# A 32-byte filler tile behind the small constants of a fused two-layer decoder trunk

## The chip, the cores and the metric

The kernel runs on one core of one Trainium2 chip. The metric is the device time of one execution in microseconds (us); a lower number is better. Times are medians of several executions. The profile is of one execution, recorded by the hardware profiler.

## The reference

The program computes two decoder layers over 1,024 tokens of width 1,024, all in float32. The first layer mixes tokens with a gated linear recurrence (HGRN2), the second with sliding-window attention of 16 query heads on 4 key/value heads; each is followed by a gated feed-forward network with a causal convolution of width 3, and every sub-layer ends in a residual sum and a layer norm:

```
for layer in range(DEPTH):                       # DEPTH = 2
    if layer < N_A_LAYERS:
        mix = hgrn2_mixer(h, hgrn_w_in[layer], lower_bounds[layer], hgrn_gnorm_w[layer], hgrn_w_out[layer])
    else:
        mix = swa_sink_mixer(h, k_shared, v_shared, swa_w_q[j], swa_sinks[j], bias, mask, swa_w_out[j])
    h = layer_norm(ALPHA * h + mix, ln_mix_g[layer], ln_mix_b[layer])
    ff = conv_ffn(h, ffn_w_in[layer], ffn_conv_w[layer], ffn_conv_b[layer], ffn_w_out[layer])
    h = layer_norm(ALPHA * h + ff, ln_ffn_g[layer], ln_ffn_b[layer])
    if layer == N_A_LAYERS - 1:
        k_flat, v_flat = jnp.split(h @ shared_w_kv, 2, axis=-1)

def conv_ffn(h, w_in, conv_w, conv_b, w_out):    # w_in (1024, 5632), w_out (2816, 1024)
    u = causal_depthwise_conv3(h @ w_in, conv_w) + conv_b
    a, b = jnp.split(u, 2, axis=-1)
    return (jax.nn.silu(a) * b) @ w_out
```

## The kernel before, in words

**Matmuls.** A float32 product is made of three fast ones. Each operand is kept as a high and a low part (the high part is a rounded copy that ScalarE, ACT in the profile, makes in `split`, L218, or `split_into`, L173; the low part is the difference that VectorE, DVE, makes in `low_part`, L166). `mm3` (L190 to L193) then issues high times high (L191), high times low (L192) and low times high (L193) into one accumulator in PSUM. So nearly all work of TensorE (PE) stands on these three lines. Each matmul first loads 128 stationary columns ("PEld" in the profile) and then streams a moving operand of 512 columns (256 in the projection of values and gates) past them. The loads of the next matmul run while the current one streams.

**Tiles.** [...] The first pool, `cp`, holds what lives for the whole program. The built program has these start addresses (bytes in the partition):

| tile | start | start modulo 64 | holds |
|---|---|---|---|
| `T` | 1,152 | 0 | the activations turned, high and low parts, 64 KB |
| `Y` | 66,688 | 0 | the activations by token, and scratch, 32 KB |
| `HL` | 99,456 | 0 | weights, high and low parts, twelve rows of 4 KB |
| `ident`, `nhalf`, `par`, `cwt`, `lbt`, `msk` | from 148,608 | 0, and 32 for `par` | identity, small constants, masks |
| tiles of `sm` | from 151,072 | 0 or 32 | small statistics of layer norm and softmax |
| all later tiles | from 152,032 | 32 | see below |

The later tiles are declared stage by stage and reuse the same space. The recurrence has `raw0` to `raw2` (landing places of weights), `V`, `G`, `A`, `Ab`, `kp`, `qp`, `kd`, `St` and others; attention has `Kh`, `Kl`, `Vt`, `X`, `q`, `W0`; the feed-forward network has `HT` (three more rows of weights, 12 KB, used like `HL`), `rx0` to `rx2` (landing places of weights), `TX` (48 KB of combined activations, three slots of high and low parts) and, in its second half, `R` and `rd`. Each of them that is 4 KB or larger starts at 32 modulo 64, and every slice of them that a matmul takes is a multiple of 512 bytes further on. The slices of `T`, `Y` and `HL` start at 0 modulo 64 in the same way.

**Order of work.** TensorE's order is written out by hand. `out_proj` (L299) multiplies the mixer's output with its output weights in two halves of 512 columns: in the first, `T` is stationary and `HL` moving, and in the second `T` is stationary and `TX` moving (the weights of `out_late` are laid into `TX` first). Then class `Up` makes the up-projection with seven block products where plain block multiplication needs eight. It loops over 22 columns of blocks `fc`. In each, `weights(fc)` loads blocks of weights into `rx` or `Y`, makes sums of them on DVE (L422 to L425) and splits them into rows of `HL` and `HT`; then seven products of twelve matmuls run in the order 1, 2, 6, 7, 4, 5, 3, each with weights stationary and activations moving. Products 1, 2, 4 and 5 stream `T`, and products 6, 7 and 3 stream `TX`. The stationary operand of 1, 2, 4 and 5 is always in `HL`; that of 6 and 7 is in `HT` when `fc` is even and in `HL` when it is odd, and that of 3 is in `HT` for every third `fc`:

```
for p in (1, 2, 6, 7, 4, 5, 3):
    self.collect(p, fc, self.product(p, fc, banks[n % 8]))
...
ws = [whole((0 if fc % 2 else 8) + i) for i in range(6)] + [whole((14, 6, 7)[fc % 3])]
```

In the last line rows up to 11 are in `HL`, and 12, 13 and 14 are in `HT`. `collect` (L444 to L476) adds the products up in `Y` on DVE and applies the convolution (L468 on ACT, L470 on DVE), the gate and the store.

Class `Down` makes the down-projection with the same seven-product scheme. There one slot of 8 KB holds both operands of a step, so that the stationary and the moving operand always come from the same tile: one of six slots of `HL`, one of `HT`, or eight of `T`, used in turn.

**Engines around it.** DVE, ACT and POOL take their instructions in the order that a scheduler or the code sets; the SP queue issues nearly all DMAs. None of this looks at an address.

Of the kernel before, what the change touches and what calls it, by code (L numbers as in the profile page):

```python
# [10 lines left out]
F32 = mybir.dt.float32  # L11
# [5 lines left out]
P = 128  # L17
# [90 lines left out]
def trunk(ctx: ExitStack, tc: tile.TileContext, a: dict, out: bass.AP):  # L108
# [5 lines left out]
    cp = ctx.enter_context(tc.tile_pool(name="cp", bufs=1))  # L114
# [11 lines left out]
    cwt = cp.tile([P, 2, 4, 2 * NF], F32, name="cwt")  # L126
    lbt = cp.tile([P, 2, NH], F32, name="lbt")
    msk = cp.tile([P, 7 * BL + P], U8, name="msk")
    h2d = drp.tile([P, 8, D], F32, name="h2d")
    ynd = drp.tile([P, 8, D], F32, name="ynd")  # L130
    gd = drp.tile([P, NF, S], F32, name="gd")
# [1347 lines left out]
def build(arrays):  # L1479
    import concourse.bacc as bacc  # L1480

    nc = bacc.Bacc("TRN2", target_bir_lowering=False, num_devices=1, dynamic_dma_scratch_size=1024)
    aps = {n: nc.dram_tensor(f"in_{n}_dram", v.shape, mybir.dt.from_np(v.dtype), kind="ExternalInput").ap()
           for n, v in arrays.items()}
    out = nc.dram_tensor("out_0_dram", (1, S, D), F32, kind="ExternalOutput").ap()
    with tile.TileContext(nc) as tc, tc.manual_schedule(engines={mybir.EngineType.PE}):
        trunk(tc, aps, out)
    return nc
# [10 lines left out]
```

## Time and profile before

| | |
|---|---|
| median of 3 runs | 2186.32 us (2185.72 to 2187.77) |
| span of the profiled execution | 2184.9 us, from its first to its last instruction |
| PE busy | 2164.9 us, 99% of the span, 13,188 matmuls |
| DVE, ACT, POOL busy | 1762.3 us (81%), 893.8 us (41%), 120.3 us (6%) |
| mean granted TensorE clock | 0.998 |
| DMA | 279.05 MB, mean 128 GB/s |

Of the profiled execution the record gives the span and no device time of its own; the median of the runs is 1.4 us above the span.

The program runs through the recurrence (0 to about 500 us of the span), its output projection (to about 577), the first up-projection (to about 1,000) and down-projection (to about 1,180), keys, values and attention (to about 1,455), and then the second output projection, up-projection (to about 1,960) and down-projection.

How to read the rows: a group of matmuls is named `line PE MATMUL out<-in`, with the two SBUF tiles that it reads, the moving one first (`TX,HL` streams `TX` past columns of `HL`; one name alone means that both are slices of that tile); the accumulator is `psmm` or `psax`. Its columns are the count, the busy time in us and the mean duration of one in ns. Matmuls are pipelined, so a duration (some 390 ns) is longer than the distance from one start to the next (some 227 ns); the distance is what adds up to the span. In a timeline the columns are start and duration in us. In rows of waits the columns are total us, times and the longest.

### The profile page before, as it was taken

Reading aid. Unit: us, or ns where it says so; the run is one execution under the profiler, and the core shown is the slowest. Engines: PE = TensorE matmul, PEld = TensorE weight load, DVE = VectorE, ACT = ScalarE, POOL = GpSimd, SP = SyncE. Lnnn points to the kernel's source line nnn. Section 1 sums busy time; section 2 is a strip of 40 time slices with the busy share of each in tenths; the row PEclk is TensorE's granted clock in tenths of the full one; section 3 lists DMA queues with packets and bytes.
Section 4 is the critical chain, followed back from the end, with each engine's and each line's share of the span. In section 5 each row is a group of like instructions: output and inputs, shape, how many; then the busy total and the mean of one; then the engine's idle time right before and its main releaser. Section 6 shows DMA issues by size and latency. Waiting matters only on the chain.

```text
span 2184.9 us, 33220 instructions
## 1 busy us (share of the span) xinstructions
PE 2164.9 (99%) x13188; PEld 1811.8 (83%) x13188; DVE 1762.3 (81%) x2388; ACT 893.8 (41%) x1457; POOL 120.3 (6%) x135
## 2 busy tenths in 40 slices
PE   9999999999999999999999999999999999999998
PEld 8888888898878888888888888878888888888887
DVE  3776665667999988888978568969999988878986
ACT  3233333342444444344433256743544444444430
POOL 1000000000100000000001123211000000000001
PEclk9999999999999999999999999999999999999999
DMA  5654533305223222228854411133223222249762
GB/s 197 232 169 161 183 136 101 99 21 175 98 75 106 87 78 81 83 97 263 290 183 155 126 32 28 32 108 115 87 96 96 79 87 77 78 139 325 235 204 94
DMA packets 229844, 279.05 MB, mean 128 GB/s; under 512 B 29960, under 2 KB 158648, under 8 KB 226872
## 3 DMA queue, kind: packets, MB, share of 16 engines
q1 hardware_dynamic: 228736, 276.53, 38.8%
q8 instruction: 104, 1.70, 0.3%
q10 hardware_dynamic: 856, 0.37, 0.1%
q14 instruction: 52, 0.43, 0.1%
q0 software_dynamic: 96, 0.02, 0.0%
HBM read 213.94 MB, written 62.94 MB: 127 GB/s over the span
## 4 chain that ended last, share of the span: by engine, by line
PE 95%; DVE 4%; ACT 1%; issue 1%; DMA 0%; SPq 0%; DVEq 0%; POOL 0%; ACTq 0%; POOLq 0%
PE psmm L191 20%; PE psmm L193 19%; PE psmm L192 19%; PE psax L192 9%; PE psax L193 9%; PE psax L191 9%; PE psax L197 3%; PE psax L201 1%; PE psmm L201 1%; PE psmm L197 1%; PE psax L1290 1%; DVE HL L166 0%; DVE T L166 0%; PE psmm L735 0%; DVE Y L470 0%
## 5 line engine op out<-in xcount | busy, mean ns | idle before, releaser
L191 PE MATMUL psmm<-T,HL 128*128 128x512 f32 x768 | 307.5, 400 | 0.0
L192 PE MATMUL psmm<-T,HL 128*128 128x512 f32 x768 | 300.3, 391 | 0.0
L193 PE MATMUL psmm<-T,HL 128*128 128x512 f32 x768 | 300.2, 391 | 0.0
L470 DVE SCALAR_TENSOR_TENSOR Y<-Y,cwt 128x1023 f32<-128x1023 f32 (+1 forms) x176 | 225.1, 1281 | 42.7 <-ACT Y L468 39.5
L218 ACT CAST HL<-rx 128x1024 fp32r<-128x1024 f32 (+1 forms) x151 | 151.0, 1004 | 199.6 <-PE psmm L192 48.8
L191 PE MATMUL psmm<-HL,T 128*128 128x256 f32 (+1 forms) x656 | 198.4, 302 | 0.0
L193 PE MATMUL psmm<-HL,T 128*128 128x256 f32 (+1 forms) x656 | 194.3, 296 | 1.4 <-DVE T L166 1.4
L192 PE MATMUL psmm<-HL,T 128*128 128x256 f32 (+1 forms) x656 | 194.0, 296 | 0.0
L166 DVE TENSOR_TENSOR HL<-rx,HL 128x1024 fp32r<-128x1024 f32 (+1 forms) x151 | 174.6, 1161 | 13.4 <-ACT HL L218 13.1
L193 PEld LDWEIGHTS psmm<-T,HL 128*128 128x128 f32 x768 | 144.2, 188 | 31.4
L191 PEld LDWEIGHTS psmm<-T,HL 128*128 128x128 f32 x768 | 144.3, 188 | 30.9 <-issue 0.8
L192 PEld LDWEIGHTS psmm<-T,HL 128*128 128x128 f32 x768 | 144.4, 188 | 28.1
L468 ACT ACTIVATE Y<-Y,cwt 128x1024 f32<-128x1024 f32 x88 | 109.0, 1238 | 103.5 <-DVE Y L457 94.4
L192 PE MATMUL psax<-T,HL 128*128 128x512 f32 x352 | 137.7, 391 | 0.0
L191 PE MATMUL psax<-T,HL 128*128 128x512 f32 x352 | 137.7, 391 | 0.0
L193 PE MATMUL psax<-T,HL 128*128 128x512 f32 x352 | 137.4, 390 | 0.0
L191 PEld LDWEIGHTS psmm<-HL,T 128*128 128x128 f32 x656 | 125.2, 191 | 6.6 <-issue 2.9
L193 PEld LDWEIGHTS psmm<-HL,T 128*128 128x128 f32 x656 | 125.2, 191 | 5.2 <-DVE T L166 2.0
L192 PEld LDWEIGHTS psmm<-HL,T 128*128 128x128 f32 x656 | 125.4, 191 | 3.3
L240 POOL TENSOR_TENSOR rs<-rs,nhalf 128x1 f32<-128x1 f32 x32 | 45.6, 1425 | 1415.4 <-DVE rs L239 1415.4
L166 DVE TENSOR_TENSOR HL<-raw,HL 128x1024 fp32r<-128x1024 f32 x51 | 62.4, 1226 | 66.9 <-ACT HL L173 66.6
L218 ACT CAST HT<-rx 128x1024 fp32r<-128x1024 f32 (+1 forms) x37 | 35.5, 959 | 114.3 <-DVE rx L424 75.1
(293 smaller groups left out, 5113.0 us busy)
## 6 DMA issues: line engine op xcount, KB each, us to landing
rx<-in_ffn_w_in_dram SPq DMA_DIRECT2D x136, 256.0 KB, 3.4
rx<-gd SPq DMA_DIRECT2D x118, 256.0 KB, 3.6
Y<-in_ffn_w_out_dram SPq DMA_DIRECT2D x44, 512.0 KB, 5.7
bsd<-Y SPq DMA_DIRECT2D x22, 1024.0 KB, 4.5
gd<-Y SPq DMA_DIRECT2D x44, 512.0 KB, 2.6
rx<-in_ffn_w_out_dram SPq DMA_DIRECT2D x54, 256.0 KB, 3.6
R<-bsd SPq DMA_DIRECT2D x44, 256.0 KB, 4.9
Y<-in_ffn_w_in_dram SPq DMA_DIRECT2D x40, 256.0 KB, 3.3
```

The source lines that it names most:

```text
L166: make = lambda e: e.tensor_tensor(lo, src, hi.bitcast(F32), op=ALU.subtract)
L191: nc.tensor.matmul(ps, st(0), mv(0), start=start, stop=False)
L192: nc.tensor.matmul(ps, st(0), mv(1), start=False, stop=False)
L193: nc.tensor.matmul(ps, st(1), mv(0), start=False, stop=stop)
L197: nc.tensor.matmul(ps, lhsT, rhs, start=start, stop=stop, **kw)
L201: nc.tensor.transpose(ps, src, ident)
L218: nc.scalar.copy(hi, src)
L240: nc.gpsimd.tensor_tensor(rs, rs, nhalf, op=ALU.pow)
L468: nc.scalar.activation(c, u, AF.Identity, bias=cwt[:, l, 3, ci:ci + 1], scale=cwt[:, l, 2, ci:ci + 1])
L470: nc.vector.scalar_tensor_tensor(c[:, sh:], u[:, :S - sh], cwt[:, l, 2 - sh, ci:ci + 1], c[:, sh:], op0=ALU.mult, op1=ALU.add)
L1290: nc.tensor.matmul(pv[:, e, jj, lo:], q[bp // 2][es, e, qs], Kl[es, pp, ks] if low else Kh[:, pp, e, ks], start=not low and jj == 0, stop= ...
```

## The change

One tile is declared at the end of the first pool's small constants. Nothing reads or writes it. It takes 32 bytes of each partition, at 151,072, so that everything that is allocated behind it moves up by 32 bytes. The later tiles now start at 152,064 and on, all of them at 0 modulo 64 where they started at 32 before; the 32-byte tiles of `sm` move from 0 to 32 and from 32 to 0. `T`, `Y`, `HL` and the constants stay where they were. The order of instructions on every engine and their waits are the same as before.

```
     lbt = cp.tile([P, 2, NH], F32, name="lbt")
     msk = cp.tile([P, 7 * BL + P], U8, name="msk")
+    edge = cp.tile([P, 8], F32, name="edge")
     h2d = drp.tile([P, 8, D], F32, name="h2d")
```

After the change, counted modulo 256 bytes, `T`, `Y` and `HL` still start at 128 and the tiles of the feed-forward network (`TX`, `HT`, `rx`, `R`, `rd`) at 0; before, these started at 224.

More of the change, by code (lines that the diff above doesn't have):

```diff
@@ L128, in trunk @@
     msk = cp.tile([P, 7 * BL + P], U8, name="msk")
+    edge = cp.tile([P, 8], F32, name="edge")
     h2d = drp.tile([P, 8, D], F32, name="h2d")
```

## The prediction

> **What bounds the kernel now.** I read the page first, then the waits of PE, and then single matmuls in the timeline.
>
> ```profile
> span 2184.9 us, 33220 instructions
> PE 2164.9 (99%) x13188; PEld 1811.8 (83%) x13188; DVE 1762.3 (81%) x2388; ACT 893.8 (41%) x1457; POOL 120.3 (6%) x135
> PE 95%; DVE 4%; ACT 1%; issue 1%; DMA 0%; SPq 0%; DVEq 0%; POOL 0%; ACTq 0%; POOLq 0%
> ```
>
> PE is busy for 99% of the span, and the chain of work that ended last runs through PE for 95%. So a microsecond saved between matmuls is a microsecond of the span, wherever PE waits for nobody. DVE, at 81%, is the only engine near it. The change touches no instruction; it can act only through the address at which something is read or written. So I look for places where the trace holds the same work at both kinds of address.
>
> Those that are not PE show nothing. Here are the low-part subtraction on DVE and the rounded copy on ACT, once from `rx` (32 modulo 64) and once from `Y` (0), and then the loads into both:
>
> ```profile
> L166 DVE TENSOR_TENSOR HL<-rx,HL 128x1024 fp32r<-128x1024 f32 x135 | 164.3, 1218 | 12.8 <-ACT HL L218 12.6 <-DMA rx<-in_ffn_w_out_dram 0.2
> L166 DVE TENSOR_TENSOR HL<-Y,HL 128x1024 fp32r<-128x1024 f32 x20 | 24.4, 1219 | 0.0
> ...
> rx<-in_ffn_w_in_dram SPq DMA_DIRECT2D x136, 256.0 KB, 3.4
> Y<-in_ffn_w_in_dram SPq DMA_DIRECT2D x40, 256.0 KB, 3.3
> ```
>
> 1218 against 1219 ns, and 3.4 against 3.3 us from issue to landing: I cost both at nothing. The 0.1 us of a load is hidden, since no DMA has a share of the chain.
>
> PE is different. The distance between starts is read from four stretches of the timeline: `T` past `HL` (both at 0 modulo 64), `TX` past `HL` (32 past 0), and `TX` past `HT` (both 32) just after PE changed over from `T`, and a little later.
>
> ```profile
> 598.92 0.39 PE L191 MATMUL psmm<-T,HL 128*128 128x512 f32 x1
> ...
> 600.96 0.40 PE L191 MATMUL psmm<-TX,HT 128*128 128x512 f32 x1
> ...
> 603.74 0.39 PE L191 MATMUL psmm<-TX,HL 128*128 128x512 f32 x1
> ...
> 605.84 0.39 PE L191 MATMUL psmm<-TX,HL 128*128 128x512 f32 x1
> ...
> 894.61 0.40 PE L191 MATMUL psmm<-TX,HT 128*128 128x512 f32 x1
> ...
> 896.70 0.39 PE L191 MATMUL psmm<-TX,HT 128*128 128x512 f32 x1
> ...
> 897.38 0.39 PE L191 MATMUL psmm<-TX,HT 128*128 128x512 f32 x1
> ...
> 899.42 0.39 PE L191 MATMUL psmm<-TX,HT 128*128 128x512 f32 x1
> ```
>
> Each pair of rows is nine starts apart. `T,HL` takes 2.04 us for nine, 226.7 ns each. `TX,HL` takes 2.10 us, 233.3 ns each, without end. `TX,HT` takes 2.09 us for the first nine after the change-over, and then 2.04 us. So it is not the 32-byte start by itself that costs: two operands that both start at 32 run as fast as two at 0. What costs is a **mixed pair**, 6.7 ns per matmul for as long as it lasts, and each **change-over** between kinds, some 0.05 us over about nine matmuls until the rhythm of 226.7 ns is back. After the change every operand of these three lines starts at 0, and neither should be left.
>
> **The change part by part.** I count the excess by the groups of the whole program. In the undisturbed group (`T` past `T` in the down-projection) a matmul lasts 389 ns; what a group's mean lies above that is its excess, since a matmul that is held back by 7 ns shows it in its duration as well (TX,HL below: 5, 7 and 9 on the three lines, 7 on average, as the timeline has it).
>
> ```profile
> L192 PE MATMUL psmm<-T 128*128 128x512 f32 x160 | 62.3, 389 | 0.0
> ...
> L193 PE MATMUL psmm<-TX,HL 128*128 128x512 f32 x160 | 63.7, 398 | 1.5 <-DVE HL L166 1.5
> L192 PE MATMUL psmm<-TX,HL 128*128 128x512 f32 x160 | 63.4, 396 | 0.0
> L191 PE MATMUL psmm<-TX,HL 128*128 128x512 f32 x160 | 63.1, 394 | 0.0
> ...
> L192 PE MATMUL psax<-TX,HL 128*128 128x512 f32 x128 | 50.7, 396 | 0.0
> L193 PE MATMUL psmm<-TX,T 128*128 128x512 f32 x128 | 50.8, 397 | 0.0
> L192 PE MATMUL psmm<-TX,T 128*128 128x512 f32 x128 | 50.6, 396 | 0.0
> L193 PE MATMUL psmm<-TX,HT 128*128 128x512 f32 x128 | 50.3, 393 | 0.0
> L192 PE MATMUL psmm<-TX,HT 128*128 128x512 f32 x128 | 50.2, 392 | 0.0
> L191 PE MATMUL psmm<-TX,HT 128*128 128x512 f32 x128 | 50.0, 390 | 0.0
> L192 PE MATMUL psax<-TX,HT 128*128 128x512 f32 x112 | 43.9, 392 | 0.0
> L192 PE MATMUL psmm<-HT 128*128 128x512 f32 x28 | 11.0, 394 | 0.0
> L192 PE MATMUL psax<-HT 128*128 128x512 f32 x16 | 6.3, 395 | 0.0
> L192 PE MATMUL psmm<-HL 128*128 128x512 f32 x164 | 64.0, 390 | 0.0
> L193 PE MATMUL psax<-HL 128*128 128x512 f32 x108 | 42.3, 392 | 0.0
> ```
>
> - `TX,HL` in the up-projections: 288 triples (160 and 128) by 9 + 7 + 5 = 21 ns, 6.0 us.
> - `TX,T` in the output projections: 128 triples by 8 + 7 and, for L191, whose own mean holds pauses between blocks, the 5 of the row above: 20 ns, 2.6 us.
> - `TX,HT`: 240 triples by 4 + 3 + 1 = 8 ns, 1.9 us. Here only the change-overs cost.
> - `HT` in the down-projections: 44 triples by 3 times 5 = 15 ns, 0.7 us. One slot in fifteen is there.
> - `HL` in the down-projections: 272 triples. Their means reach from 389 to 392; 1.5 ns per matmul, 4.5 a triple, 1.2 us. These follow a slot in `HT`.
>
> There remain the `T,HL` products, that follow `TX` in the up-projections. In the first one's stretch (588 to 1,000 us) they show:
>
> ```profile
> L192 PE MATMUL psmm<-T,HL 128*128 128x512 f32 x176 | 68.9, 391 | 0.0
> L191 PE MATMUL psmm<-T,HL 128*128 128x512 f32 x176 | 68.7, 390 | 0.0
> ...
> L192 PE MATMUL psax<-T,HL 128*128 128x512 f32 x160 | 62.6, 391 | 0.0
> ```
>
> 336 triples by 2 + 1 + 1 = 4 ns (L193 is taken as L191) are 1.3 us, and 2.7 us for both layers. The `T,HL` of the recurrence and of attention never meet `TX`; they are disturbed by stops and by small matmuls, and I leave them as they are.
>
> The sum is 6.0 + 2.6 + 1.9 + 0.7 + 1.2 + 2.7 = **15.1 us** off PE's own time. The transposes and the small matmuls of recurrence and attention show no price of this kind that I can name, and are costed at nothing. From above, the `T,HL` of the recurrence could go as well; its stretch (0 to 500 us) shows
>
> ```profile
> L192 PE MATMUL psmm<-T,HL 128*128 128x512 f32 x256 | 100.0, 391 | 0.0
> ```
>
> 2 ns by three lines by 256 triples, 1.5 us, and I add half of that for attention: 2.3 us at most.
>
> **What PE cannot keep.** Where DVE has no idle time, a faster PE only waits longer for it. That is so from the second half of the first output projection to the start of the up-projection's loop. (First the stretches' rows: PE, PEld, DVE, ACT and POOL busy; then DVE and PE in the timeline.)
>
> ```profile
> 601.00:643.00 42.00, 42.00 (x183) 33.94 (x181) 40.37 (x46) 21.83 (x23) 0.00 (x0) 1.00 0.18 59
> 643.00:720.00 77.00, 76.25 (x332) 62.26 (x332) 74.87 (x86) 34.85 (x40) 0.00 (x0) 1.00 0.35 109
> ...
> 637.15 0.69 DVE L462 TENSOR_TENSOR Y<-Y,psax 128x512 f32<-128x512 f32 x1 [0.39 <-PE psax L193]
> ...
> 643.81 0.50 PE L193 MATMUL psmm<-TX,HL 128*128 128x512 f32 x1 [0.75 <-DVE HL L166]
> ...
> 1562.74 0.69 DVE L451 TENSOR_TENSOR Y<-Y,psmm 128x512 f32<-128x512 f32 x1 [2.02 <-PE psmm L193]
> ```
>
> DVE is busy for 40.37 of 42 us, waits 0.39 us for PE, and PE then stands 0.75 us for DVE's weights. PE would come to that point earlier by 1.3 us (half of `TX,T`) and 0.5 us (42 us of the loop; its 10.6 us over two times 425 us are 0.0125 per us), but DVE at best by the 0.39 and what little it idles ahead of that (1.6 us in the whole stretch, whatever it waits for). I take 1.3 of these 1.8 us as lost. In the second layer DVE waits 2.02 us for PE ahead of the same stretch, so the 1.3 comes through, and only 0.2 is lost. From 643 to 720 PE would need 76.25 - 1.0 = 75.3 us and DVE 74.87: nearly level. Between nothing and 1.0 us is lost there per layer; 0.4 each, since PE has eight accumulators to run ahead into. Further on DVE has room (the page has it at 81% over the span). Lost in all: 1.3 + 0.2 + 0.8 = 2.3 us.
>
> So the span goes from 2184.9 to 2184.9 - 15.1 + 2.3 = 2172.1 us. The median lies 1.4 us above the profiled span; with that kept, **2173.5 us**. With none lost it is 2171.2, with 4.4 lost (1.8 + 0.6 + 2.0) 2175.6, and with none lost and the 2.3 us of the recurrence and attention gone as well 2168.9.
>
> **The rivals.**
>
> 1. *The unit isn't 64 bytes.* All pairs in the trace that run at 226.7 ns are at a distance of a multiple of 512 bytes from each other; those at 233.3 are 96 (modulo 256) apart. After the change `TX` and `HT` are 128 (modulo 256) from `T` and `HL`, a distance that no pair of the trace has. If the rhythm needs equal starts modulo 128 or less, the price goes; if it needs 256, everything stays, and the time is 2186 us. The size of the step speaks for the small unit. In the undisturbed group above 512 columns last 389 ns, and 256 columns last
>
> ```profile
> L192 PE MATMUL psmm<-HL,T 128*128 128x256 f32 x576 | 162.8, 283 | 0.0
> ```
>
>    283 ns, so that 256 columns take 106 ns, or 0.41 ns a column. 6.7 ns are 16 columns, 64 bytes of float32.
> 2. *The steady price goes and the change-over stays*, because it comes with the tile and not with the address. Then `TX,HL` and `TX,T` fall only to the level of `TX,HT`, 8 ns a triple: 416 triples by 12 to 13 ns are 5.2 us, less some 1 us lost to DVE, 2182 us. For it: each change-over is also a change of tile. Against: change-overs from one slot of `HL` to one of `T` in the down-projection leave `T` at 389.
> 3. *Slower.* The new distance of 128 bytes collides worse than 96 did: place, the same 416 mixed triples; price, another step of 20 ns each, 8.3 us, to about 2194 us. It decides if the memory behind the two streams is laid out in units over 64 bytes. In its favour is only that the distance is untried.
> 4. *The start has no part in it*, and `TX` is slow by something that goes with it, such as what DVE and ACT write meanwhile. Then nothing changes, 2186 us. Against it: `TX` past `HT` runs at 226.7 ns at 897 us, with DVE and ACT as busy as ever.
>
> [...]
>
> **How the numbers follow.** Forecast 0.81; rival 1 0.05, rival 2 0.06, rival 3 0.05, rival 4 0.03. The likeliest time is 2173.5 us. The range is 2168 to 2180 us: it takes in the bounds of the forecast, 2168.9 to 2175.6, and goes part of the way to rival 2, for a loss to DVE that is larger than I see. 0.2% is 4.4 us, about what a measurement of this kernel can tell from no change; faster by more than that are the forecast and half of rival 2 (0.84), within it rivals 1 and 4 and the rest of rival 2 (0.11), slower rival 3 (0.05). Rivals 1 to 4, 0.19 together, lie outside the range.
>
> **What would show it.** In the changed kernel's groups `TX,HL`, `TX,T`, `TX,HT` and `HT` should all stand at 389 to 390 ns, and nine starts of `TX,HL` should take 2.04 us. PE's wait for the weights of L166 near 643 us should grow by about a microsecond in the first layer and by less in the second. DVE, ACT and the DMAs should keep their durations. A `TX,HL` at 396 with a `TX,HT` at 392 would be rival 1 or 4, both near 392 rival 2, above 400 rival 3. If the groups fall to 389 and the span doesn't, DVE bounds more of the up-projection than I allow.

## The result, and the profile after

The changed kernel took 2180.97 us (median of 6 runs, 2179.98 to 2181.87), the kernel before 2187.46 us beside it (6 runs, 2185.72 to 2188.72). The ratio is 0.9971, with a 95% interval of 0.9959 to 0.9982: faster by 6.5 us, half of the 12.8 us that were forecast. The profiled execution took 2180.73 us, its span 2178.9 us.

The head of its page, with the share of the chain of work by engine:

```profile
span 2178.9 us, 33220 instructions
PE 2158.8 (99%) x13188; PEld 1812.8 (83%) x13188; DVE 1761.6 (81%) x2388; ACT 893.8 (41%) x1457; POOL 119.8 (5%) x135
PE 94%; DVE 4%; ACT 1%; issue 1%; DMA 0%; SPq 0%; POOL 0%; DVEq 0%; ACTq 0%; POOLq 0%
```

PE's busy time fell by 6.1 us (2164.9 to 2158.8) and the span by 6.0 (2184.9 to 2178.9). So what left PE's own time reached the end nearly whole. What is missing was never taken off PE. The groups of matmuls say which part (the added line moves the numbers up by one: L192, L193 and L194 are L191 to L193 of before):

```profile
L194 PE MATMUL psmm<-TX,HL 128*128 128x512 f32 x160 | 63.4, 396 | 1.6 <-DVE HL L167 1.6
L192 PE MATMUL psmm<-TX,HL 128*128 128x512 f32 x160 | 63.1, 395 | 0.0
L193 PE MATMUL psmm<-TX,HL 128*128 128x512 f32 x160 | 63.1, 394 | 0.0
...
L194 PE MATMUL psmm<-TX,T 128*128 128x512 f32 x128 | 50.6, 395 | 0.0
...
L193 PE MATMUL psmm<-TX,T 128*128 128x512 f32 x128 | 50.5, 395 | 0.0
L194 PE MATMUL psmm<-TX,HT 128*128 128x512 f32 x128 | 50.0, 391 | 0.0
L192 PE MATMUL psmm<-TX,HT 128*128 128x512 f32 x128 | 49.9, 390 | 0.0
L193 PE MATMUL psmm<-TX,HT 128*128 128x512 f32 x128 | 49.8, 389 | 0.0
```

`TX,HL`, forecast at 389, stands at 394 to 396 (394 to 398 before), and `TX,T` at 395. `TX,HT` went from 390, 392 and 393 to 390, 389 and 391. So the steady price of a mixed pair stayed and most of the change-over price left. In the timeline the same:

```profile
601.10 0.39 PE L192 MATMUL psmm<-TX,HT 128*128 128x512 f32 x1
...
603.14 0.39 PE L192 MATMUL psmm<-TX,HT 128*128 128x512 f32 x1
...
603.83 0.40 PE L192 MATMUL psmm<-TX,HL 128*128 128x512 f32 x1
...
605.93 0.39 PE L192 MATMUL psmm<-TX,HL 128*128 128x512 f32 x1
```

The first nine starts of `TX,HT` behind `T` now take 2.04 us, where they took 2.09. Nine starts of `TX,HL` still take 2.10 us, 233.3 ns each, although both tiles start at 0 modulo 64. The `T,HL` of the first up-projection (588 to 1,000 us) lost most of the excess that followed a change-over:

```profile
L193 PE MATMUL psmm<-T,HL 128*128 128x512 f32 x176 | 68.6, 390 | 0.0
L192 PE MATMUL psmm<-T,HL 128*128 128x512 f32 x176 | 68.5, 389 | 0.0
...
L192 PE MATMUL psax<-T,HL 128*128 128x512 f32 x163 | 63.5, 389 | 0.0
```

391 and 390 became 390 and 389. What the change was forecast to leave alone, it did: DVE's low part takes 1217 ns from `rx` and 1218 from `Y`, and ACT's rounded copy from `rx` 1050 (1049 before).

### The profile page after: what moved, and what is told of

Read it like the earlier page. It is cut to its first block, busy times and chain, and to the rows that moved or that the text cites. A ratio compares the mean times of both kernels' runs of the same rounds, so it can differ in the third digit from the quotient of the medians.

```text
span 2178.9 us, 33220 instructions
## 1 busy us (share of the span) xinstructions
PE 2158.8 (99%) x13188; PEld 1812.8 (83%) x13188; DVE 1761.6 (81%) x2388; ACT 893.8 (41%) x1457; POOL 119.8 (5%) x135
## 4 chain that ended last, share of the span: by engine, by line
PE 94%; DVE 4%; ACT 1%; issue 1%; DMA 0%; SPq 0%; POOL 0%; DVEq 0%; ACTq 0%; POOLq 0%
PE psmm L192 20%; PE psmm L194 19%; PE psmm L193 19%; PE psax L192 9%; PE psax L194 9%; PE psax L193 9%; PE psax L198 3%; PE psax L202 1%; PE psmm L202 1%; PE psmm L198 1%; PE psax L1291 1%; DVE HL L167 0%; DVE T L167 0%; PE psmm L736 0%; DVE Y L471 0%
## 5 line engine op out<-in xcount | busy, mean ns | idle before, releaser
L192 PE MATMUL psmm<-T,HL 128*128 128x512 f32 x768 | 307.4, 400 | 0.0
L194 PE MATMUL psmm<-T,HL 128*128 128x512 f32 x768 | 299.9, 390 | 0.0
L193 PE MATMUL psmm<-T,HL 128*128 128x512 f32 x768 | 299.3, 390 | 0.0
L192 PE MATMUL psmm<-HL,T 128*128 128x256 f32 (+1 forms) x656 | 198.4, 302 | 0.0
L194 PE MATMUL psmm<-HL,T 128*128 128x256 f32 (+1 forms) x656 | 194.3, 296 | 1.4 <-DVE T L167 1.4
L193 PE MATMUL psmm<-HL,T 128*128 128x256 f32 (+1 forms) x656 | 194.0, 296 | 0.0
L194 PEld LDWEIGHTS psmm<-T,HL 128*128 128x128 f32 x768 | 144.1, 188 | 31.2
L192 PEld LDWEIGHTS psmm<-T,HL 128*128 128x128 f32 x768 | 144.2, 188 | 30.2 <-issue 0.8
L193 PEld LDWEIGHTS psmm<-T,HL 128*128 128x128 f32 x768 | 144.5, 188 | 27.6
L192 PE MATMUL psax<-T,HL 128*128 128x512 f32 x352 | 137.5, 391 | 0.0
L194 PE MATMUL psax<-T,HL 128*128 128x512 f32 x352 | 137.2, 390 | 0.0
L193 PE MATMUL psax<-T,HL 128*128 128x512 f32 x352 | 137.1, 390 | 0.0
L192 PEld LDWEIGHTS psmm<-HL,T 128*128 128x128 f32 x656 | 125.3, 191 | 6.5 <-issue 2.9
L194 PEld LDWEIGHTS psmm<-HL,T 128*128 128x128 f32 x656 | 125.2, 191 | 5.2 <-DVE T L167 2.1
L193 PEld LDWEIGHTS psmm<-HL,T 128*128 128x128 f32 x656 | 125.4, 191 | 3.2
```

Of the source, the lines that this page charges most:

```text
L192: nc.tensor.matmul(ps, st(0), mv(0), start=start, stop=False)
L193: nc.tensor.matmul(ps, st(0), mv(1), start=False, stop=False)
L194: nc.tensor.matmul(ps, st(1), mv(0), start=False, stop=stop)
```

## The experiments

**What was to be told apart.** Is it the start of a tile modulo 64, or the difference between the starts of the two operands, and then modulo what? In each experiment fillers alone are changed; no instruction is. In the text and the table the difference is that of the feed-forward network's tiles (`TX`, `HT`) minus `T` and `HL`, counted modulo 256: +96 before, +128 after the change. (Two of the expectations below give it as a distance modulo 512, without its sign.) The built program's addresses show the step in which starts can be shifted: from `ident` at 148,608 to the first tile of `sm` at 151,072 the constants take 2,464 bytes, where their sizes sum to 2,408; `nhalf`, of 4 bytes, takes 32, and `par`, of 68, takes 96.

**Equal starts.** First with a filler that puts all large tiles at 128 modulo 512, and then with one that makes them equal modulo 256 and not modulo 512:

```
-    edge = cp.tile([P, 8], F32, name="edge")
+    edge = cp.tile([P, 40], F32, name="edge")
```

> The filler is 160 bytes: T, Y, HL and all tiles of the feed-forward network start at 128 modulo 512. Distance theory (a pair of operands costs when their starts differ modulo 512): TX,HL, TX,T, TX,HT and HT fall to 389 to 390 ns, nine starts of TX,HL take 2.04 us, and the time is 2187.5 - 15.1 + 2.3 = 2174.7 us, 0.994 of before. Tile theory (TX is slow whatever its start): TX,HL stays at 394 to 396 and the time at 2181 us, 0.997.

```
-    edge = cp.tile([P, 8], F32, name="edge")
+    edge = cp.tile([P, 104], F32, name="edge")
```

> The filler is 416 bytes: T, Y and HL start at 128 modulo 512, the later tiles at 384, so that the starts are equal modulo 256 and differ by 256 modulo 512. If the distance counts modulo 256: as the filler of 160 bytes, 0.994 of before, TX,HL at 389. If it counts modulo 512: TX,HL stays at 394 to 396 and the time at about 0.997. Tile theory: 0.997 too.

They took 2170.81 and 2171.40 us beside 2187.05 of before: ratios 0.9928 (0.9914 to 0.9942) and 0.9925 (0.9911 to 0.9939). The first one's page, groups and timeline:

```profile
span 2168.8 us, 33220 instructions
PE 2148.6 (99%) x13188; PEld 1811.5 (84%) x13188; DVE 1760.1 (81%) x2388; ACT 895.1 (41%) x1457; POOL 119.9 (6%) x135
```

```profile
L194 PE MATMUL psmm<-TX,HL 128*128 128x512 f32 x160 | 62.5, 390 | 1.6 <-DVE HL L167 1.6
L193 PE MATMUL psmm<-TX,HL 128*128 128x512 f32 x160 | 62.3, 389 | 0.0
L192 PE MATMUL psmm<-TX,HL 128*128 128x512 f32 x160 | 62.3, 389 | 0.0
...
L193 PE MATMUL psmm<-TX,T 128*128 128x512 f32 x128 | 49.8, 389 | 0.0
L192 PE MATMUL psmm<-TX,HT 128*128 128x512 f32 x128 | 49.8, 389 | 0.0
```

```profile
603.67 0.39 PE L192 MATMUL psmm<-TX,HL 128*128 128x512 f32 x1
...
605.71 0.39 PE L192 MATMUL psmm<-TX,HL 128*128 128x512 f32 x1
```

Everything that the prediction said of the change is here: 389 and 390 in these groups, and 2.04 us for nine starts of `TX,HL`. Equal modulo 256 is enough, since in the second kernel `TX,HL` and `TX,HT` read 389 and 390 as well.

One thing in that span is not the change's. At the end of attention PE stands still for DVE twice (1.43 and 1.55 us before, 1.42 and 1.55 here), and in the executions of before and after the granted clock then falls for a short time (0.81 on average from 1,447 to 1,456 us of before and from 1,444 to 1,453 of after); in this execution it is 1.00 at that place (1,440 to 1,449 us). The same step, first of before and then of this kernel:

```profile
1446.92 1.12 PE L197 MATMUL psmm<-W,Vt 128*64 128x128 f32 x16 [1.43 <-DVE W L1329]
...
1455.75 1.15 PE L197 MATMUL psmm<-Y,Vt 128*64 128x128 f32 x16
```

```profile
1440.38 1.11 PE L198 MATMUL psmm<-W,Vt 128*64 128x128 f32 x16 [1.42 <-DVE W L1330]
...
1447.72 1.15 PE L198 MATMUL psmm<-Y,Vt 128*64 128x128 f32 x16
```

8.83 us became 7.34. So 1.5 of the 16.1 us between the two spans are the clock's, and 14.6 remain for equal starts.

**Other differences.** A filler of 96 bytes gives +192, one of 64 bytes +160.

```
-    edge = cp.tile([P, 8], F32, name="edge")
+    edge = cp.tile([P, 24], F32, name="edge")
```

> The filler is 96 bytes: the later tiles start at 64 modulo 512, a multiple of 64, at a distance of 64 from T and HL. Distance theory: TX,HL stays at 394 to 398. If a distance that is a multiple of 64 is what shortened the change-overs in the changed kernel: TX,HT at 389 to 391 and about 0.997 of before. If it was the distance of 128 alone: TX,HT at 390 to 393 and 0.997 to 1.000.

```
-    edge = cp.tile([P, 8], F32, name="edge")
+    edge = cp.tile([P, 16], F32, name="edge")
```

> The filler is 64 bytes: the later tiles start at 32 modulo 512, at a distance of 96 from T and HL, which is no multiple of 64 as in the kernel before (distance 160). Distance theory: TX,HL at 394 to 398. If the multiple of 64 shortens change-overs: TX,HT at 390 to 393 as before and 1.000 of before, within 0.001. If not: anything from 0.997 to 1.000, unlike before.

2182.97 us (0.9981, 0.9972 to 0.9991) and 2185.51 us (0.9992, 0.9983 to 1.0001), beside the same 2187.05. Groups of +192:

```profile
L194 PE MATMUL psmm<-TX,HL 128*128 128x512 f32 x160 | 63.3, 396 | 1.5 <-DVE HL L167 1.5
L193 PE MATMUL psmm<-TX,HL 128*128 128x512 f32 x160 | 63.1, 394 | 0.0
L192 PE MATMUL psmm<-TX,HL 128*128 128x512 f32 x160 | 63.1, 394 | 0.0
...
L193 PE MATMUL psmm<-TX,HT 128*128 128x512 f32 x128 | 49.9, 390 | 0.0
L194 PE MATMUL psmm<-TX,HT 128*128 128x512 f32 x128 | 49.9, 390 | 0.0
L192 PE MATMUL psmm<-TX,HT 128*128 128x512 f32 x128 | 49.8, 389 | 0.0
```

The steady price is about the same at +192 as at +128 (17 and 18 ns over the three lines): it didn't shrink with the distance, which is 64 here. Nor is it a matter of 64 bytes: 192 is a multiple of it. Change-overs are cheap here as in the changed kernel (`TX,HT` at 389 to 391 in both), and at +160 they are not (389, 392 and 392).

**Is it the start itself, or the difference?** One kernel puts every large tile at 32 modulo 64, all at 224 modulo 256. The other has `T` and `Y` at 128 and `HL` with all later tiles at 224, so that the pairs change places: `T,HL` is mixed, `TX,HL` is equal.

```
+    head = cp.tile([P, 88], F32, name="head")
...
-    edge = cp.tile([P, 8], F32, name="edge")
+    edge = cp.tile([P, 40], F32, name="edge")
```

> A filler of 352 bytes ahead of T and one of 160 behind the constants: T, Y, HL and the tiles of the feed-forward network all start at 224 modulo 256, so at 32 modulo 64, at equal starts modulo 256. Distance theory (only the difference of the two starts modulo 256 counts): as the fillers of 160 and 416 bytes, 0.993 of before, TX,HL at 389. If the multiple of 64 itself has a part: slower than those by 0.2% or more, with all groups above 389.

```
+    mid = cp.tile([P, 88], F32, name="mid")
...
-    edge = cp.tile([P, 8], F32, name="edge")
+    edge = cp.tile([P, 40], F32, name="edge")
```

> A filler of 352 bytes between Y and HL and one of 160 behind the constants: HL and the later tiles at 224 modulo 256, T and Y at 128. Now T past HL and HL past T are the mixed pairs, TX past HL and TX past HT are equal, TX past T is mixed as before. Distance theory: T,HL and HL,T rise from 390 to 391 to 394 to 398 (1120 and 128 triples by some 13 to 20 ns more, 16 to 25 us), TX,HL falls to 389 (288 triples by 21 ns, 6 us back), and the 256-column HL,T may rise too; time 1.004 to 1.012 of before. If TX is slow for another reason than its distance: T,HL stays at 390 to 391 and the time within 0.997 to 1.000.

The first filler lies ahead of `T`, the second between `Y` and `HL`. They took 2171.26 us (0.9929, 0.9915 to 0.9944) and 2198.54 us (1.0051, 1.0034 to 1.0067) beside 2187.14. With all at 32 modulo 64 the kernel is as fast as with all at 0 (2171.26 against 2170.81 and 2171.40 us): at equal starts the multiple of 64 has no part in it. Of the second, the groups (two lines were added, so the lines are L193 to L195):

```profile
L193 PE MATMUL psmm<-T,HL 128*128 128x512 f32 x768 | 311.8, 406 | 0.0
L195 PE MATMUL psmm<-T,HL 128*128 128x512 f32 x768 | 304.1, 396 | 0.0
L194 PE MATMUL psmm<-T,HL 128*128 128x512 f32 x768 | 303.9, 396 | 0.0
...
L194 PE MATMUL psmm<-HL,T 128*128 128x256 f32 x576 | 161.7, 281 | 0.0
...
L194 PE MATMUL psmm<-TX,HL 128*128 128x512 f32 x160 | 62.4, 390 | 0.0
```

`T,HL` went from 400, 391 and 391 to 406, 396 and 396, and `TX,HL` from 394 to 398 down to 390 and 391. Here the price followed the difference to the pair that has it. The 128 triples of `HL,T` with 512 columns rise as well, where the other operand is the moving one (399, 392 and 390 in `psmm` become 402, 397 and 396). Only the products of 256 columns (`HL,T`) do not show it: 283 before on L192, 281 here, at a difference of 96.

**The rest of the circle.** The hypothesis left for the change-overs was that a difference of a multiple of 64 makes them cheap. Three more fillers give +32, +64 and +224:

```
-    edge = cp.tile([P, 8], F32, name="edge")
+    edge = cp.tile([P, 48], F32, name="edge")
```

> The filler is 192 bytes: the tiles of the feed-forward network start 32 bytes behind T and HL modulo 256, the smallest difference that the pool can make, and at 32 modulo 64. Any difference costs the same (the steady price is a yes or no): TX,HL at 394 to 398, and with the long change-overs of a difference that is no multiple of 64 0.998 to 1.000 of before. The price grows with the difference: TX,HL nearer 390 and the time at 0.993 to 0.996.

```
-    edge = cp.tile([P, 8], F32, name="edge")
+    edge = cp.tile([P, 56], F32, name="edge")
```

> The filler is 224 bytes: the later tiles start 64 bytes behind T and HL modulo 256, a multiple of 64. Steady price yes or no: TX,HL at 394 to 396. Change-overs short at every multiple of 64: TX,HT at 389 to 391 and 0.997 to 0.998 of before. Change-overs short only at 128 and 192: TX,HT at 390 to 393 and 0.999 to 1.000.

```
-    edge = cp.tile([P, 8], F32, name="edge")
+    edge = cp.tile([P, 32], F32, name="edge")
```

> The filler is 128 bytes: the later tiles start 224 bytes behind T and HL modulo 256, no multiple of 64. Steady price yes or no: TX,HL at 394 to 398. Change-overs long where the difference is no multiple of 64: TX,HT at 390 to 393 and 0.998 to 1.000 of before. If the difference works only in one direction or by its size: anything down to 0.994, with TX,HL below 394.

2183.62 us (0.9985, 0.9975 to 0.9995), 2180.20 us (0.9971, 0.9959 to 0.9983) and 2185.39 us (0.9992, 0.9983 to 1.0002), beside 2186.71. Groups of +64:

```profile
L192 PE MATMUL psmm<-TX,HL 128*128 128x512 f32 x160 | 63.1, 394 | 0.0
L194 PE MATMUL psmm<-TX,HL 128*128 128x512 f32 x160 | 62.9, 393 | 1.5 <-DVE HL L167 1.5
L193 PE MATMUL psmm<-TX,HL 128*128 128x512 f32 x160 | 62.5, 390 | 0.0
...
L192 PE MATMUL psmm<-TX,HT 128*128 128x512 f32 x128 | 50.2, 392 | 0.0
L194 PE MATMUL psmm<-TX,HT 128*128 128x512 f32 x128 | 50.1, 392 | 0.0
...
L193 PE MATMUL psmm<-TX,HT 128*128 128x512 f32 x128 | 49.8, 389 | 0.0
```

The hypothesis falls: at +64 the change-overs are dear (392 twice), and here it is the steady price that is about halved. All differences together, as the sum over the three lines of what a matmul lasts above 389 ns, into `psmm`:

| difference | kernel | `TX,HL`, ns | `TX,HT`, ns | median, us (ratio to before) |
|---|---|---|---|---|
| 0 | `edge` of 160 bytes | 1 | 0 | 2170.81 (0.9928) |
| +32 | 192 bytes | 21 | 5 | 2183.62 (0.9985) |
| +64 | 224 bytes | 10 | 6 | 2180.20 (0.9971) |
| +96 | before | 21 | 8 | |
| +128 | after, 32 bytes | 18 | 3 | 2180.97 (0.9971) |
| +160 | 64 bytes | 23 | 6 | 2185.51 (0.9992) |
| +192 | 96 bytes | 17 | 2 | 2182.97 (0.9981) |
| +224 | 128 bytes | 22 | 6 | 2185.39 (0.9992) |

Each of the seven differences other than 0 costs something in both columns (10 to 23 and 2 to 8 ns); +128, where the change has put the tiles, is one of the cheaper ones. The two columns do not order the times fully: +192 has the smaller entries and a median 2.0 us above that of +128. The busy time of `T,HL`, 1319.0 us at +192 and 1318.4 at +128, has 0.6 us of that; the rest was not traced.

## Why the prediction was wrong

- **The bound was right.** PE's own time is the span's: 6.1 and 6.0 us in the changed kernel, 16.3 and 16.1 us with equal starts.
- **The step that failed** is the sentence "After the change every operand of these three lines starts at 0, and neither should be left". It takes 64 bytes as the unit. The only support was a length of time, 6.7 ns or 16 columns, and a length of time is not a unit of addresses. Of the eight differences that were run only 0 modulo 256 left `TX,HL` without the price (1 ns over the three lines, 10 to 23 at the other seven). That is the case of rival 1 ("if it needs 256, everything stays"), which the prediction gave 0.05 although it had noted that no pair of the trace had the new distance of 128.
- **But not everything stayed**, and so rival 1's 2186 us was wrong as well. The difference also sets the price of a change-over, and at +128 it is low (`TX,HT` in the table: from 8 to 3 ns). The terms, from the busy times of the groups in us:

| term | forecast | after | equal starts (`edge` of 160 bytes) |
|---|---|---|---|
| `TX,HL` | 6.0 | 1.2 | 5.8 |
| `TX,T` | 2.6 | 0.2 | 2.0 |
| `TX,HT` | 1.9 | 1.6 | 2.0 |
| `HT` in the down-projections | 0.7 | 0.3 | 0.7 |
| `HL` in the down-projections | 1.2 | 0.6 | 0.9 |
| `T,HL` | 2.7 | 2.4 | 3.6 |
| sum | 15.1 | 6.3 | 15.0 |

  Each entry is the sum of a group's three busy times before less that after, `psmm` and `psax` together (`TX,HL` into `psmm` went from 63.1 + 63.4 + 63.7 to 63.1 + 63.1 + 63.4, that is 0.6, and into `psax` 0.6 more). `T,HL` is counted over the whole program, its 2.7 over the up-projections alone, where the prediction left 2.3 us of the recurrence and attention as a bound. The two terms of steady price, forecast at 8.6 us, gave 1.4; the four of change-overs, forecast at 6.5, gave 4.9. In the last column the forecast's sizes hold to 0.1 us in sum, and in part because errors cancel: `TX,T` gave 0.6 less than forecast, and `T,HL` 0.9 more (3.0 us of its 3.6 in the up-projections, matmul by matmul, against 2.7). So the steps were about rightly sized; they belong to a filler that makes the starts equal.
- **The loss to DVE was sized too large**, 2.3 us. The wait that should have grown by about a microsecond near 643 us did not. First of after, then with equal starts:

```profile
643.77 0.50 PE L194 MATMUL psmm<-TX,HL 128*128 128x512 f32 x1 [0.79 <-DVE HL L167]
```

```profile
643.17 0.50 PE L194 MATMUL psmm<-TX,HL 128*128 128x512 f32 x1 [0.81 <-DVE HL L167]
```

  It was 0.75 us at 643.81. With equal starts PE came 0.64 us earlier, and DVE's weights with it. Something was lost ahead of that point, inside the output projection. The same two matmuls of before and then with equal starts:

```profile
566.02 0.39 PE L192 MATMUL psmm<-TX,T 128*128 128x512 f32 x1
...
573.75 0.48 PE L191 MATMUL psmm<-TX,T 128*128 128x512 f32 x1
```

```profile
565.57 0.39 PE L193 MATMUL psmm<-TX,T 128*128 128x512 f32 x1
...
573.42 0.66 PE L202 MATMUL psmm<-ident,Y 128*128 128x128 f32 x4 [0.17 <-ACT Y L376]
573.84 0.47 PE L192 MATMUL psmm<-TX,T 128*128 128x512 f32 x1
```

  PE's lead over before falls from 0.45 us to -0.09, at the two sets of transposes (`ident,Y`) in between; for the second set PE waits for ACT. That is a loss of 0.54 us, where the sum (15.0 us) and the spans (14.6 without the clock's part) differ by 0.4; the small rest was not traced. From 588 us, where the lead is 0.01, to 1,000 us it grows to 5.81 us, so nothing of note is lost there, and in the second layer the same stretches show no such loss (1.2 us gained up to 1,560 us, 5.8 from there to 1,960).
- **Rival 2** had the two prices the wrong way round: the steady one should go and the change-over stay. That its 2182 us lies next to the measured 2180.97 is chance. **Rival 3** was right that the distance of 128 is no free one and wrong that it is worse: `TX,HL` costs 18 ns there, 21 at +96. **Rival 4**, by which the starts have no part, is refuted by the experiments: the same instructions took 2170.81, 2180.97 and 2198.54 us. The time hangs on both operands together: nine starts of `TX,HL` take 2.04 us at equal starts modulo 256, and 2.10 us at +96 and at +128.

## What to carry to other kernels

When a matmul group's mean stands a few ns above that of a like group, compare the start addresses of its two operands: here equal starts modulo 256 bytes ran at 226.7 ns per 512 columns, and each of the seven other differences tried cost something, about 3% (233.3 ns) at +96 and +128, which a filler of the right size between tiles removed. A distance at which the trace shows a price says nothing of a distance that it doesn't show; if one is to be forecast from the other, the unit needs at least two distances, and without them the rival "another unit" deserves a large chance.

## What the runs showed of the hardware that was not expected

The price has two parts that do not go together: at +64 the steady part is half (10 ns per triple against 17 to 23) and the change-over dear (6 ns), at +128 and +192 it is the other way round (18 and 17 ns, 3 and 2). Matmuls of 256 columns showed no steady price at the one difference tried, 96 (283 ns before, 281 with `T,HL` mixed). Only starts and durations were seen; why the starts of the two operands count together, and why modulo 256 bytes, was not shown and stays open.

After PE stood still for DVE near 1,445 us, the granted clock fell in the profiled executions of before and after (0.81 over 9 us) and not in that with equal starts (1.00), worth 1.5 us. By an estimate an average of 0.81 over 9 us is what 3.4 us at half speed would give; from 1,449.6 us of before, four transposes take 1.09 us where they take 0.63 with equal starts, and `HL,T` matmuls behind them start 0.43 us apart instead of 0.23, up to 1,452.6. What brings the fall was not shown. Executions of one kernel differ in the mean clock as well: with equal starts (`edge` of 160 bytes) it is 0.999 in three (2170.56 to 2170.81 us) and 0.998 in two (2172.96 and 2173.01 us), at +224 0.999 in five (2182.43 to 2185.59 us) and 0.997 in three (2185.78 to 2186.47 us). So the difference of starts alone does not set it, and a difference of 1.5 us between two single executions, and between two neighbouring medians of the table above too, needs the clock beside it.
